# A hybrid encoder layer in fp32: the feed-forward's gate and up blocks taken in pairs, the norm's weights moved into h, one set of weight buffers

## The chip, the core and the metric

The kernel runs on one core of a Trainium2 chip. The metric is the device time of one execution in microseconds (us). PE is the matrix engine (TensorE), PEld its loads of stationary operands, DVE the vector engine (VectorE), ACT the scalar engine (ScalarE), POOL is GpSimd, and SP (SyncE) issues most transfers; SPq, PEq and so on are the queues of these engines.

## The reference

One layer over 256 tokens of width 2048, all in float32. What matters here:

```python
u = rms_norm(h, g_pre_mix);  proj = u @ w_in            # 2048 x 5120, three kinds of mixers behind it
h = h + rms_norm(mixed @ w_out, g_post_mix)             # 2048 x 2048
u = rms_norm(h, g_pre_ffn)
f = silu(u @ w_gate) * (u @ w_up)                       # 2048 x 5632 each
h = h + rms_norm(f @ w_down, g_post_ffn)                # 5632 x 2048
```

## The kernel before, in words

Activations are the stationary operand (128 x 128 tiles; two token tiles t = 0, 1) and weights the moving one (128 x 512). Every float32 product is made of three fp32r matmuls: high part by high part, high by low, low by high. So each weight block, an **item** of 256 rows x 512 columns (512 KB), takes 2 token tiles x 2 row tiles x 3 = 12 matmuls.

All items stand in one list, `stream`, in the order in which PE uses them: 80 of `w_in`, 32 of `w_out`, then the feed-forward's 11 blocks of 512 columns with 8 gate items and 8 up items each, then `w_down`. An item is loaded by SP into one of four raw buffers (`load`), cast to its high part `hi` by ACT and subtracted to its low part `lo` by DVE (`prep`) into one of five pairs, and taken by PE. In the feed-forward `prep` works in halves, since each row tile is scaled by its own column of `g_pre_ffn` (L240, L241); everywhere else one cast and one subtraction do the whole 128 x 1024 (L244, L246).

ACT, DVE and PE each run their instructions in the order in which the program writes them down (`manual_schedule`). Everything else (norms, mixers, silu, transposes) is written as side jobs, generators that are continued in `side.slot()` after each item as far as a budget of DVE and ACT time goes; `side.need(job)` continues slots until that job is written out, with no item of PE between.

In the down projection four pairs of k blocks (`SFORM`) are already done with seven products in place of eight (`seven`): the weights' sums are made by DVE (L226), the activations' sums in the feed-forward's last step.

Between `w_out` and the feed-forward stands a stretch written out by hand (the **h stage**): `h_part` makes h = x + normed output, `h_turn` transposes it on PE, `h_hi` casts it (ACT, out of PSUM), `h_lo` makes the low part (DVE). The gate items of block 0 are used there already. `h_job` then sums the squares of h on ACT (L418) for the norm's factor `rffn`. After the last up item `up_job` multiplies silu(gate) by up, transposes the result on PE and splits it for the down projection.

At the start `start_job` loads x transposed (`xT`, k tiles 8 to 11 and 12 to 15 as one transfer each) and then x itself in two halves.

Of the kernel before, what the change touches and what calls it, by code (L numbers as in the profile page):

```python
# [10 lines left out]
F32 = mybir.dt.float32  # L11
# [22 lines left out]
NRAW = 4  # L34
NPARTS = 5
# [25 lines left out]
class Side:  # L61
# [18 lines left out]
    def slot(self):  # L80
        self.n += 1
        self.left = [min(left + rate, self.MOST) for left, rate in zip(self.left, self.RATE)]
# [22 lines left out]
class Std:  # L105


    def __init__(self, ap, b=None, n=None):
        self.ap, self.b, self.n = ap, b, n
        self.has_load = True  # L110


class Prod:


    def __init__(self, group, name, ap, dst, add, frees):
        self.group, self.name, self.ap, self.dst, self.add, self.frees = group, name, ap, dst, add, frees
        self.has_load = ap is not None
        self.added = add is None


def seven(w11, w12, w21, w22, **at):

    g = {"bufs": {}, **at}
    return [
        Prod(g, "Q3", w22, "y", None, ""),  # L130
        Prod(g, "P7", w12, "x", ("x", "x", "y", ALU.add), ""),
        Prod(g, "P1", w11, "z", None, ""),
        Prod(g, "P6", None, "x", ("x", "x", "z", ALU.add), "z"),
        Prod(g, "P2", w21, "u", None, ""),
        Prod(g, "Q5", None, "y", ("y", "x", "y", ALU.subtract), "y"),
        Prod(g, "R4", None, "x", ("x", "x", "u", ALU.add), "xu"),
    ]

# [33 lines left out]
def block_kernel(ctx, tc, xT, x_tok, params, w_in, w_out, w_gate, w_up, w_down, lru_w, g_post, g_post2, out):  # L172
# [18 lines left out]
    for cs in ((6, 7), (0, 1, 2, 3), (4, 5)):  # L191
        stream += [w_out[b, c] for b in range(4) for c in cs]
    for i in range(NFB):
        stream += [w_gate[i, c] for c in range(8)] + [w_up[i, c] for c in range(8)]
    stream = [Std(ap) for ap in stream]
    gate0 = (len(mixers) + 4) * 8
    down0 = gate0 + NFB * 16
    plain = [n for n in range(NFK // 2) if n // 2 not in SFORM]
    downs = []
    for b, head, tail in ((0, 6, 4), (2, 3, 8)):  # L200
        prods = [p for i in SFORM for p in seven(*(w_down[b + c, 2 * i + k] for k, c in ((0, 0), (0, 1), (1, 0), (1, 1))), i=i)]
        downs.append(mingled(prods, [Std(w_down[b + c, n], b + c, n) for c in range(2) for n in plain], head, tail))
    stream += downs[0] + downs[1]
    early = range(gate0 + 1, gate0 + 1 + NEARLY)
    raws, parts = {}, {}
    at = {"load": 0, "prep": 0, "use": 0, "done": 0}

    sraws = Shelf([])

    def load(i, raw=None):  # L210
        item = stream[i]
        if isinstance(item, Prod):
            if item.has_load:
                buf = item.group["bufs"][item.dst] = sraws.lend(NT, CB)
# [5 lines left out]
    def add(i):  # L220

        item = stream[i] if i < len(stream) else None
        if isinstance(item, Prod) and not item.added and i < at["load"]:
            dst, a, b, op = item.add
            bufs = item.group["bufs"]
            V.tensor_tensor(out=bufs[dst], in0=bufs[a], in1=bufs[b], op=op)  # L226
            item.added = True

    def prep(i, tiles=None):
        item = stream[i]  # L230
        if isinstance(item, Prod):
            add(i)
            raw = item.group["bufs"][item.dst]
        else:
            raw = raws.pop(i)
        hi, lo = tiles or (wp.tile([P, 2, CB], F32R, tag=n, name=n, bufs=NPARTS) for n in ("hi", "lo"))
        if gate0 <= i < down0:
            for kk in range(2):
                g = pv("g_pre_ffn", (i - gate0) % 8 * 2 + kk)
                A.activation(hi[:, kk, :], raw[:, kk, :], AF.Copy, scale=g)  # L240
                V.scalar_tensor_tensor(out=lo[:, kk, :], in0=raw[:, kk, :], scalar=g, in1=hi[:, kk, :].bitcast(F32),  # L241
                                       op0=ALU.mult, op1=ALU.subtract)
        else:
            A.copy(out=hi, in_=raw)  # L244
            add(i + 1)
            V.tensor_tensor(out=lo, in0=raw, in1=hi.bitcast(F32), op=ALU.subtract)  # L246
        parts[i] = (hi, lo)
        if isinstance(item, Prod):
            for n in item.frees:
                sraws.back(item.group["bufs"].pop(n))  # L250

    def load_next():
        while at["load"] in early:
            at["load"] += 1
        if at["load"] < min(len(stream), at["prep"] + NRAW):
            item = stream[at["load"]]
            if isinstance(item, Prod) and item.has_load and not sraws.free:
                return False
            load(at["load"])
# [4 lines left out]
    def top_up_one():  # L264
# [10 lines left out]
        load_next()  # L275
        if i >= down0:
            while load_next():
                pass
# [11 lines left out]
    def release():  # L290
        at["done"] += 1
        top_up()

# [32 lines left out]
    later = const.tile([P, P], F32, name="later")  # L326
    G.affine_select(out=later, in_=ones, pattern=[[-1, P]], compare_op=ALU.is_ge, fill=0.0, base=0, channel_multiplier=1)
# [14 lines left out]
    xt = res.tile([P, NT, D], F32, tag="xt", name="xt")  # L342
# [1092 lines left out]
```

## Time and profile before

| | before |
|---|---|
| median of 3 runs | 1075.41 us (1074.4 to 1076.36) |
| the profiled execution's own time | 1075.32 us |
| its span | 1073.6 us |
| busy: PE, DVE, ACT | 1060.2, 769.4, 634.5 us |
| 128 x 512 matmuls written in the program | 4472 |

The span is what the trace covers; some 1.7 us of the execution lie around it. A PE row's busy time overlaps the next row's, since matmuls are pipelined: what a matmul costs is read from the distance between starts.

### The profile page before, as it was taken

To read this page: it belongs to the slowest core of one execution; us is meant where nothing else is said; L and a number is where in the kernel's file an instruction comes from. 1 tells how busy PE (TensorE), PEld (TensorE's weight loads), DVE (VectorE), ACT (ScalarE), POOL (GpSimd) and SP (SyncE) were. 2 spreads that over 40 slices of the span, in tenths; PEclk is the share of its full clock that TensorE was granted. 3 is DMA by queue.
4 is the path that set the end of the run, shared out by engine and by line. 5 is a ranking of instruction groups with operands and counts; after the bars stand their busy time and mean duration, and the time that the engine had idled before them with its cause. 6 is when DMAs were issued, how large, how long until landed. Compare 5 with 4: busy or idle time off the path is not lost.

```text
span 1073.6 us, 13241 instructions
## 1 busy us (share of the span) xinstructions
PE 1060.2 (99%) x4778; PEld 878.5 (82%) x4778; DVE 769.4 (72%) x1088; ACT 634.5 (59%) x901; POOL 7.8 (1%) x19
## 2 busy tenths in 40 slices
PE   8999999999999999999999999999999999999996
PEld 6888888888888888888888888888888888888885
DVE  6576998986688775765565665566655688788885
ACT  6778757678854855555464564555554455555552
POOL 0000000010000000000000000000000000000000
PEclk9999999999999999999999999999999999999998
DMA  8865554656563775565665556556556456656662
GB/s 313 279 197 175 193 169 153 194 167 215 204 230 104 248 234 185 177 206 185 196 185 188 196 183 193 193 177 197 194 191 237 162 197 223 230 170 196 223 230 79
DMA packets 58385, 211.21 MB, mean 197 GB/s; under 512 B 6480, under 2 KB 6864, under 8 KB 57552
## 3 DMA queue, kind: packets, MB, share of 16 engines
q1 hardware_dynamic: 58320, 210.38, 59.3%
q8 instruction: 37, 0.61, 0.2%
q14 instruction: 28, 0.23, 0.1%
HBM read 206.16 MB, written 4.19 MB: 196 GB/s over the span
## 4 chain that ended last, share of the span: by engine, by line
PE 96%; DMA 1%; DVE 1%; ACT 0%; SPq 0%; issue 0%; DVEq 0%; ACTq 0%
PE acc L297 24%; PE acc L298 24%; PE acc L299 24%; PE acc L1375 4%; PE acc L1374 4%; PE acc L1373 4%; PE bank L1375 3%; PE bank L1374 3%; PE bank L1373 3%; PE bank L1211 1%; DMA raw<-w_in 1%; DMA w<-xT 1%; PE bank L442 1%; DVE xt L1303 0%; PE bank L1065 0%; PE bank L752 0%
## 5 line engine op out<-in xcount | busy, mean ns | idle before, releaser
L297 PE MATMUL acc<-hi,w 128*128 128x512 f32 x1008 | 396.3, 393 | 1.5 <-DVE w L428 1.5
L298 PE MATMUL acc<-lo,w 128*128 128x512 f32 x1008 | 393.7, 391 | 0.3 <-DVE lo L861 0.3
L299 PE MATMUL acc<-hi,w 128*128 128x512 f32 x1008 | 393.6, 390 | 0.0
L241 DVE SCALAR_TENSOR_TENSOR lo<-raw,par,hi 128x512 fp32r<-128x512 f32 x344 | 242.8, 748 | 170.2 <-ACT hi L240 170.0
L240 ACT ACTIVATE hi<-raw,par 128x512 fp32r<-128x512 f32 x344 | 229.7, 718 | 193.2 <-PE acc L299 185.8
L246 DVE TENSOR_TENSOR lo<-raw,hi 128x1024 fp32r<-128x1024 f32 x166 | 202.2, 1225 | 85.9 <-ACT hi L244 84.5
L244 ACT CAST hi<-raw 128x1024 fp32r<-128x1024 f32 x166 | 172.5, 1048 | 127.6 <-PE acc L299 51.3
L297 PEld LDWEIGHTS acc<-hi,w 128*128 128x128 f32 x1008 | 189.9, 188 | 40.9 <-ACT hi L860 2.4
L299 PEld LDWEIGHTS acc<-hi,w 128*128 128x128 f32 x1008 | 189.8, 188 | 40.1 <-DVE w L1072 0.5
L298 PEld LDWEIGHTS acc<-lo,w 128*128 128x128 f32 x1008 | 189.8, 188 | 40.0 <-DVE lo L861 1.2
L244 ACT CAST hi<-w 128x1024 fp32r<-128x1024 f32 x56 | 58.6, 1053 | 41.7 <-DVE w L226 21.9
L246 DVE TENSOR_TENSOR lo<-w,hi 128x1024 fp32r<-128x1024 f32 x56 | 68.1, 1224 | 11.2 <-ACT hi L244 8.7
L1373 PE MATMUL acc<-hi,w 128*128 128x512 f32 x156 | 60.8, 390 | 0.0
L1375 PE MATMUL acc<-hi,w 128*128 128x512 f32 x156 | 60.7, 389 | 0.0
L1373 PE MATMUL bank<-hi,w 128*128 128x512 f32 x156 | 60.7, 389 | 0.0
L1374 PE MATMUL bank<-lo,w 128*128 128x512 f32 x156 | 60.7, 389 | 0.0
L1375 PE MATMUL bank<-hi,w 128*128 128x512 f32 x156 | 60.7, 389 | 0.0
L1374 PE MATMUL acc<-lo,w 128*128 128x512 f32 x156 | 60.7, 389 | 0.0
L684 DVE SCALAR_TENSOR_TENSOR w<-u,par,w 128x256 f32<-128x256 f32 x120 | 51.6, 492 | 0.0
L297 PE MATMUL acc<-hi,mh 128*128 128x512 f32 x128 | 50.4, 394 | 0.0
L299 PE MATMUL acc<-hi,ml 128*128 128x512 f32 x128 | 49.9, 390 | 0.0
L298 PE MATMUL acc<-lo,mh 128*128 128x512 f32 x128 | 49.8, 389 | 0.0
(252 smaller groups left out, 854.9 us busy)
## 6 DMA issues: line engine op xcount, KB each, us to landing
raw<-w_up SPq DMA_DIRECT2D x88, 512.0 KB, 3.5
raw<-w_gate SPq DMA_DIRECT2D x84, 512.0 KB, 4.1
raw<-w_in SPq DMA_DIRECT2D x78, 512.0 KB, 3.5
raw<-w_down SPq DMA_DIRECT2D x56, 512.0 KB, 3.5
raw<-w_out SPq DMA_DIRECT2D x32, 512.0 KB, 3.8
w<-w_down SPq DMA_DIRECT2D x32, 512.0 KB, 4.8
xt<-x_tok SPq DMA_DIRECT2D x2, 1024.0 KB, 8.1
w<-g_post SPq DMA_DIRECT2D x4, 512.0 KB, 5.3
```

What stands on the lines that cost most here:

```text
L240: A.activation(hi[:, kk, :], raw[:, kk, :], AF.Copy, scale=g)
L241: V.scalar_tensor_tensor(out=lo[:, kk, :], in0=raw[:, kk, :], scalar=g, in1=hi[:, kk, :].bitcast(F32), op0=ALU.mult, op1=ALU.subtract)
L244: A.copy(out=hi, in_=raw)
L246: V.tensor_tensor(out=lo, in0=raw, in1=hi.bitcast(F32), op=ALU.subtract)
L297: T.matmul(acc, xh(k)[:, ts], hi[:, kk, :], start=first, stop=False)
L298: T.matmul(acc, xh(k)[:, ts], lo[:, kk, :], start=False, stop=False)
L299: T.matmul(acc, xl(k)[:, ts], hi[:, kk, :], start=False, stop=last)
L442: T.transpose(out=b[:, c * P:(c + 1) * P], in_=src[:, t, c * P:(c + 1) * P], identity=ident)
L684: V.scalar_tensor_tensor(out=cy[:, n, :], in0=u[:, n, j:j + S], scalar=pv("dw_conv_w", j * 4 + n), in1=cy[:, n, :], op0=ALU.mult, op1=ALU.add)
L1373: T.matmul(out_bank, xhi, hi[:, kk, :], start=n == first[to] and kk == 0, stop=False)
L1374: T.matmul(out_bank, xhi, lo[:, kk, :], start=False, stop=False)
L1375: T.matmul(out_bank, xlo, hi[:, kk, :], start=False, stop=n == end[to] and kk == 1)
```

## The change

For blocks 1 to 10 the first 512 rows of the gate block and of the up block beside it are taken as one 2 x 2 matrix of 256 x 512 weight blocks (rows by gate/up) against the 2 x 2 of two token tiles by 256 rows of h, and multiplied with seven products (`seven_in_turn`): P1, P6, P7, Q5, P2, R4, Q3, each of 6 matmuls, in place of eight. That is 42 matmuls for 48, ten times: 4412 in the program for 4472. P1, P6 and P7 are running sums in one PSUM bank, which ACT copies out after each of them (L1397); P1, P6, P7 of a block are done among the up items of the block before. Sums of weights are made by DVE in `prep` (L259, 128 x 1024, four for each pair), sums of h once (`forms`).

For this h must hold the norm's weights itself, or the sums would mix rows with different weights. For columns 1024 to 2047 of h (b = 2, 3) `h_hi` now multiplies by `g_pre_ffn` on DVE (L1112) before the cast. For b = 0, 1 block 0 still runs with weights scaled in `prep`, and then `regain_job` rebuilds h from its two parts (L1255, DVE), scales it (L1258, ACT), splits it again, and for b = 0 makes the forms of h, all while the up items of block 0 run; P1 of block 1 is written behind both jobs (`side.need(*regain)`). Items of later blocks are split with one cast and one subtraction (L274, L276).

Raw buffers are one set, `weights`: four, and the three places of x once h is saved; a load may run six items ahead (`AHEAD`), and several are issued in one go. h is saved by GpSimd's queue. The forms of f go to DRAM and come back. x is loaded as four strips of columns.

```diff
-NRAW = 4
+AHEAD = 6
...
+def seven_in_turn(w11, w12, w21, w22, **at):
+    return dict([
+        item("P1", "z", "", ("z", w11), ("y", w22)),
+        item("P6", "z", "", ("x", w12), pre=[("x", "x", "y", ALU.add)], post=[("z", "z", "x", ALU.add)]),
+        item("P7", "x", ""),
+        item("Q5", "x", "x", pre=[("x", "z", "y", ALU.subtract)]),
+        item("P2", "u", "", ("u", w21)),
+        item("R4", "z", "zu", pre=[("z", "z", "u", ALU.add)]),
+        item("Q3", "y", "y"),
+    ])
...
+        if i:
+            q = sevens[i]
+            ffn += [*g[:2], q["Q5"], g[2], q["P2"], *g[3:5], q["R4"], g[5], q["Q3"]]
+        if i == 0:
+            q = sevens[1]
+            ffn += [*u[:6], q["P1"], u[6], q["P6"], u[7], q["P7"]]
+        elif i + 1 < NFB:
+            q = sevens[i + 1]
+            ffn += [*u[:-4], q["P1"], u[-4], q["P6"], *u[-3:-1], q["P7"], u[-1]]
...
-        if at["load"] < min(len(stream), at["prep"] + NRAW):
+        if i < min(len(stream), at["prep"] + AHEAD) and len(weights.free) >= len(stream[i].loads):
...
-        load_next()
-        if i >= down0:
-            while load_next():
-                pass
+        while load_next():
+            pass
...
     def h_hi(t, b):
-        A.copy(out=hh[b][:, :, t * P:(t + 1) * P], in_=turned[t, b].rearrange("p (c t) -> p c t", c=4))
+        bank = turned[t, b].rearrange("p (c t) -> p c t", c=4)
+        if b >= 2:
+            h = shelf.lend(4, P)
+            g = par[:, POFF["g_pre_ffn"] + 4 * b:POFF["g_pre_ffn"] + 4 * (b + 1)]
+            V.tensor_tensor(out=h, in0=bank, in1=g.rearrange("p (c t) -> p c t", t=1).broadcast_to([P, 4, P]), op=ALU.mult)
+            banks.back(turned[t, b])
+            bank = turned[t, b] = h
+        A.copy(out=hh[b][:, :, t * P:(t + 1) * P], in_=bank)
...
+    def forms(dst, a11, a12, a21, a22):
+        s1, s2, s3, s4 = (dst[:, n:n + 2, :] for n in (0, 2, 4, 6))
+        V.tensor_tensor(out=s1, in0=a21, in1=a22, op=ALU.subtract)
+        V.tensor_tensor(out=s2, in0=s1, in1=a11, op=ALU.subtract)
+        V.tensor_tensor(out=s4, in0=s2, in1=a12, op=ALU.add)
+        V.tensor_tensor(out=s3, in0=a11, in1=a21, op=ALU.subtract)
...
+    def regain_job(b):
+        while ("used", b) not in st:
+            yield WAIT
+        h = xplaces[b](4, S)
+        yield 1.2, 0, 0
+        V.tensor_tensor(out=h, in0=hh[b].bitcast(F32), in1=hl[b].bitcast(F32), op=ALU.add)
+        yield 0, 2.0, 0
+        for n in range(4):
+            A.activation(h[:, n, :], h[:, n, :], AF.Copy, scale=pv("g_pre_ffn", 4 * b + n))
+        yield 1.2, 1.05, 0
+        split(hh[b], hl[b], h)
+        if b == 0:
+            s = xplaces[2](8, P)
+            yield 1.9, 0, 0
+            forms(s, *quarters(h))
+            yield 1.0, 0.9, 0
+            split(*hform, s[:, 2:8, :])
+            yield 0.5, 0.4, 0
+            split(hh[0][:, 0:2, P:], hl[0][:, 0:2, P:], s[:, 0:2, :])
...
+    def ffn_after(item, full):
+        dst = {"P1": p1, "P6": p16, "Q5": q5}.get(item.name)
+        if item.name == "P7":
+            dst = p167[i % 2]
+        if dst is not None:
+            A.copy(out=dst, in_=accs[(i, 1, 1) if item.name == "Q5" else (i, 0, 1)])
...
+    run(ffn, ffn_uses, ffn_bank, ffn_after)
...
+    side.need(last_up)
```

On SP, at the start of the program: the two long transfers of xT (`w_196`, `w_232` before; `w_204`, `w_240` after) among the loads of `w_in`, each of which waits for the raw buffer that it fills. Before:

```order
L218 DMA raw_188<-w_in 128x1024 [waits DMAHW4_49,DVE_49]
L422 DMA w_196<-xT 128x1024 [waits DMAHW5_49]
L218 DMA raw_202<-w_in 128x1024 [waits DMAHW7_49,DMAHW6_49,DVE_49]
L218 DMA raw_208<-w_in 128x1024 [waits DMAHW1_49,DVE_49]
L422 DMA w_232<-xT 128x1024 [waits DMAHW0_49]
L218 DMA raw_238<-w_in 128x1024 [waits DMAHW3_49,DVE_49]
```

After:

```order
L252 DMA w_192<-w_in 128x1024 [waits DMAHW4_49,DVE_49]
L252 DMA w_194<-w_in 128x1024 [waits DMAHW7_49,DMAHW5_49,DVE_49]
L252 DMA w_196<-w_in 128x1024 [waits DMAHW6_49,DMAHW1_49,DVE_49]
L465 DMA w_204<-xT 128x1024
L252 DMA w_210<-w_in 128x1024 [waits DMAHW3_49,DMAHW0_49,DVE_49]
L252 DMA w_216<-w_in 128x1024 [waits DMAHW4_49,DVE_49]
L465 DMA w_240<-xT 128x1024 [waits DMAHW2_49]
```

The first xT transfer has moved behind two loads that wait for DVE, the second behind one that waits for a later step of DVE than before.

On ACT, in the up stage of block 0. Before, behind the gate's sigmoid (L1193) stand only the casts of the coming items, two halves each:

```order
L1193 ACTIVATE w_3377<-acc_3106,rffn_90 128x512 [waits DVE_49]
L1193 ACTIVATE w_3377<-acc_3107,rffn_90 128x512
L240 ACTIVATE hi_3399<-raw_3257,par_72 128x512 [waits DMAHW6_49,PE_49]
L240 ACTIVATE hi_3399<-raw_3257,par_72 128x512
L240 ACTIVATE hi_3421<-raw_3287,par_72 128x512 [waits DMAHW7_49,PE_49]
L240 ACTIVATE hi_3421<-raw_3287,par_72 128x512
L240 ACTIVATE hi_3441<-raw_3315,par_72 128x512 [waits DMAHW1_49,PE_49]
```

After, from the cast of P1's weights (`w_3319`, later P6's) to the first copy out of P1's bank (`acc_3531`). `w_3426` is h's columns 0 to 511 and `w_3477` columns 512 to 1023, `w_3434` the forms; `w_3343`, `w_3461` are up items 6 and 7, `w_3410` is P7's weights. Ahead of these rows stand the cast of up item 5 and the scaling and cast of `w_3426`:

```order
L274 CAST hi_3435<-w_3319 128x1024 [waits DMAHW7_49,PE_49]
L274 CAST hi_3455<-w_3343 128x1024 [waits DMAHW1_49,PE_49]
L1235 CAST w_3384<-w_3434 128x768 [waits DVE_49]
L274 CAST hi_3478<-w_3319 128x1024 [waits DVE_49,PE_49]
L1235 CAST w_3001<-w_3434 128x2x128 [waits Activation_49]
L1258 ACTIVATE w_3477<-w_3477,par_72 128x256 [waits DMASW1_49,DVE_49]
L1258 ACTIVATE w_3477<-w_3477,par_72 128x256 x3
L274 CAST hi_3501<-w_3461 128x1024 [waits DMAHW4_49,PE_49]
L1235 CAST w_3002<-w_3477 128x1024 [waits Activation_49]
L274 CAST hi_3525<-w_3410 128x1024 [waits PE_49]
L1397 COPY w_3386<-acc_3531 128x512 [waits PE_49]
```

The copy out of P1's bank, which PE needs before it can start P6 in that bank, stands behind a dozen other instructions, among them the whole second rebuild of h.

On PE, where the feed-forward ends: the transposes of the last f (L1211, L1306), from the bank `w_3377` or `w_3383`. Before, 48 matmuls of the down projection (L1373 to L1375; the last four are shown) stand between the last up item and them:

```order
L1375 MATMUL acc_7025<-hi_6991,w_3368 128x512
L1373 MATMUL acc_7025<-hi_6991,w_3357 128x512
L1374 MATMUL acc_7025<-lo_6992,w_3357 128x512
L1375 MATMUL acc_7025<-hi_6991,w_3368 128x512
L1211 MATMUL bank_7093<-ident_73,w_3377 128x128 [waits DVE_49,PE_49]
L1211 MATMUL bank_7093<-ident_73,w_3377 128x128 x3
L1211 MATMUL bank_7098<-ident_73,w_3377 128x128 [waits DVE_49]
L1211 MATMUL bank_7098<-ident_73,w_3377 128x128 x3
L1373 MATMUL acc_7024<-hi_7009,w_3359 128x512 [waits Activation_49]
```

After, with the last four matmuls of the last up item (L326 to L328, `acc_6668`), and behind them the first of the down projection (`acc_6962`):

```order
L328 MATMUL acc_6668<-hi_6823,w_2904 128x512
L326 MATMUL acc_6668<-hi_6823,w_3004 128x512
L327 MATMUL acc_6668<-lo_6824,w_3004 128x512
L328 MATMUL acc_6668<-hi_6823,w_2904 128x512
L1306 MATMUL bank_6932<-ident_73,w_3383 128x128 [waits DVE_49,PE_49]
L1306 MATMUL bank_6932<-ident_73,w_3383 128x128 x3
L1306 MATMUL bank_6937<-ident_73,w_3383 128x128 [waits DVE_49,PE_49]
L1306 MATMUL bank_6937<-ident_73,w_3383 128x128 x3
L326 MATMUL acc_6962<-hi_6841,w_3361 128x512 [waits Activation_49]
```

The transposes have moved up to stand directly behind the item whose result they turn.

## Rows read from the trace of the kernel before

**Rows 1.** Busy time of each engine, share of the span, instructions (the page's part 1).

```profile
PE 1060.2 (99%) x4778; PEld 878.5 (82%) x4778; DVE 769.4 (72%) x1088; ACT 634.5 (59%) x901; POOL 7.8 (1%) x19
```

**Rows 2.** PE's waits: line, releaser, us in total, times, longest.

```profile
PE acc L297 <- DVE w L428: 1.5, 1, 1.5
```

**Rows 3.** Timeline of PE: start us, us, line, out<-in (x8: eight in a row).

```profile
399.20 0.39 PE L297 MATMUL acc<-hi,w 128*128 128x512 f32 x1
399.43 0.39 PE L298 MATMUL acc<-lo,w 128*128 128x512 f32 x1
...
400.57 1.04 PE L1211 MATMUL bank<-ident,w 128*128 128x128 f32 x8
```

**Rows 4.** The chain in order of time: the transposes of two neighbouring blocks.

```profile
400.74 0.88 PE bank L1211 x8
...
445.14 0.88 PE bank L1211 x8
```

**Rows 5.** Costliest groups (part 5): line, shapes xcount | busy us, mean ns | idle before.

```profile
L241 DVE SCALAR_TENSOR_TENSOR lo<-raw,par,hi 128x512 fp32r<-128x512 f32 x344 | 242.8, 748 | 170.2 <-ACT hi L240 170.0
...
L246 DVE TENSOR_TENSOR lo<-raw,hi 128x1024 fp32r<-128x1024 f32 x166 | 202.2, 1225 | 85.9 <-ACT hi L244 84.5
L244 ACT CAST hi<-raw 128x1024 fp32r<-128x1024 f32 x166 | 172.5, 1048 | 127.6 <-PE acc L299 51.3
```

**Rows 6.** Busy us of each engine by stretch: h stage, feed-forward, down projection.

```profile
core 0: us, PE busy (x) PEld busy (x) DVE busy (x) ACT busy (x) POOL busy (x), PEclk, DMA share, GB/s
352.00:364.00 12.00, 12.00 (x61) 9.96 (x60) 12.00 (x19) 10.20 (x20) 0.00 (x0) 1.00 0.63 206
404.00:448.00 44.00, 44.00 (x200) 36.53 (x199) 26.00 (x39) 22.57 (x34) 0.00 (x0) 1.00 0.59 191
...
1020.00:1063.00 43.00, 43.00 (x191) 35.61 (x191) 31.45 (x41) 20.97 (x26) 0.00 (x0) 1.00 0.38 144
```

**Rows 7.** Timeline of SP's queue at the start.

```profile
8.84 0.52 SPq L422 DMA_DIRECT2D w<-xT  x1
11.34 3.67 SPq L218 DMA_DIRECT2D raw<-w_in  x2
15.06 0.43 SPq L422 DMA_DIRECT2D w<-xT  x1
```

**Rows 8.** Timelines of ACT, DVE and PE behind the second xT transfer.

```profile
22.17 1.71 ACT L430 ACTIVATE w<-w,par 128x256 fp32r<-128x256 f32 x4 [2.68 <-DMA w<-xT]
23.79 3.88 ACT L244 CAST hi<-raw 128x1024 fp32r<-128x1024 f32 x4
...
24.86 4.63 DVE L246 TENSOR_TENSOR lo<-raw,hi 128x1024 fp32r<-128x1024 f32 x4 [0.46 <-ACT hi L244]
...
20.23 0.39 PE L297 MATMUL acc<-hi,w 128*128 128x512 f32 x1
```

**Rows 9.** Timelines of ACT and DVE, PE at k tile 14: end of the h stage.

```profile
359.73 1.05 ACT L1068 CAST w<-bank 128x512 fp32r<-128x512 f32 x2
...
375.25 5.14 ACT L240 ACTIVATE hi<-raw,par 128x512 fp32r<-128x512 f32 x8
...
361.51 1.29 DVE L1072 TENSOR_TENSOR w<-bank,w 128x512 fp32r<-128x512 f32 x2
...
365.20 0.39 PE L297 MATMUL acc<-hi,w 128*128 128x512 f32 x1
```

**Rows 10.** Timelines of PE and DVE, windows (busy, PEclk, DMA share): PE's first and last matmuls.

```profile
9.51 0.63 PE L297 MATMUL acc<-hi,w 128*128 128x512 f32 x1
9.94 0.63 PE L298 MATMUL acc<-lo,w 128*128 128x512 f32 x1
...
1063.13 0.39 PE L1375 MATMUL bank<-hi,w 128*128 128x512 f32 x1
...
1064.24 0.68 DVE L1264 TENSOR_TENSOR w<-bank,w 128x512 f32<-128x512 f32 x1
...
1067.00:1070.00 3.00, 0.00 (x0) 0.00 (x0) 2.86 (x8) 0.00 (x0) 0.00 (x0) 0.50 0.24 89
```

More of the change, by code (lines that the diff above doesn't have):

```diff
@@ L34 @@
 NRAW = 4
+AHEAD = 6
+READ = ("P1", "P6", "P7", "Q5")
 NPARTS = 5
@@ L102, in need, with __init__ @@
             self.slot()
[L105 to L119, printed above, removed]
+class Item:
+    def __init__(self, bufs, loads, src, frees, pre=(), post=(), **where):
+        self.bufs, self.loads, self.src, self.frees = bufs, loads, src, frees
+        self.sums = {"pre": list(pre), "post": list(post)}
+        self.__dict__.update(where)
@@ L220, in add @@
[L220 to L227, printed above, removed]
+        for name, ap in item.loads:
+            item.bufs[name] = weights.lend(NT, CB) if raw is None else raw
+            nc.sync.dma_start(out=item.bufs[name], in_=ap)
@@ L237, in prep @@
[L237 to L242, printed above, removed]
+        sums(i, "pre")
+        sums(i, "post")
+        raw = item.bufs[item.src]
+        hi, lo = tiles or (wp.tile([P, 2, CB], F32R, tag=n, name=n, bufs=NPARTS) for n in ("hi", "lo"))
@@ L247, in prep @@
         parts[i] = (hi, lo)
-        if isinstance(item, Prod):
-            for n in item.frees:
-                sraws.back(item.group["bufs"].pop(n))
+        if not tiles:
+            weights.back(*(item.bufs.pop(n) for n in item.frees))
     def load_next():
@@ L292, in release, with six @@
         top_up()
+    def six(bank, tiles, w, first, last, again=False):
+        hi, lo = w
+        for kk in range(2):
+            xhi, xlo = tiles[kk]
+            T.matmul(bank, xhi, hi[:, kk, :], start=first and kk == 0, stop=False, skip_group_check=again)
+            T.matmul(bank, xhi, lo[:, kk, :], start=False, stop=False, skip_group_check=again)
+            T.matmul(bank, xlo, hi[:, kk, :], start=False, stop=last and kk == 1, skip_group_check=again)
     def product(acc, x, k, t, w, kk, first, last):
@@ L879, in block_kernel @@
     shelf.back(x0)
-    raws.clear()
+    weights.back(*(stream[i].bufs.pop("w") for i in range(2)))
     load_x(x1, 4, 2)
@@ new lines, in block_kernel, with ffn_uses, ffn_bank @@
+    accs, added = {}, {}
+    def ffn_uses(item):
+        if item.name is None:
+            return [((item.i, item.col, t), part_tiles(hidden, 2 * item.c, t)) for t in range(NT)]
+        to = {"P2": (0, 0), "Q3": (1, 0), "Q5": (1, 1)}.get(item.name, (0, 1))
+        return [((item.i, *to), of_product(item.name, hidden, hform))]
+    def ffn_bank(item, to):
+        if to not in accs:
+            i, col, _ = to
+            if i == 1 and col == 0:
+                side.need(*regain)
+            if i:
+                side.need(*(added[n] for n in ((i - 1, 0),) if n in added))
+                while col and ("up", i - 1) not in st:
+                    side.slot()
+            accs[to] = ps.tile([P, CB], F32, tag="acc", name="acc", bufs=4)
+        return accs[to]
@@ L1247, in block_kernel @@
+    added[0, 0] = side.add(0, silu_job(0, acc))
+    regain = [side.add(1, regain_job(b)) for b in range(2)]
+    run(ffn, ffn_uses, ffn_bank, ffn_after)
+    last_up = added[NFB - 1, 1]
     y2 = [[None] * 4 for _ in range(NT)]
@@ L1316, in std_form @@
[L1316 to L1327 removed]
+    sforms = {}
@@ new lines, in bring_back_job, with down_uses @@
+    def bring_back_job():
+        for b in (3, 0, 1, 2):
+            while b < 3 and xplaces[b] not in weights.free:
+                yield WAIT
+            if b < 3:
+                weights.free.remove(xplaces[b])
+            kept[b] = xplaces[b](NT, CB)
+            G.dma_start(out=kept[b], in_=hsave[b])
+        yield 0, 0, 0
+    yjobs, ybanks, sjobs = [], {}, {}
+    own = []
+    def down_uses(item):
+        if item.name is None:
+            return [((item.b, t), part_tiles(ff, 2 * item.n, t)) for t in range(NT)]
+        to = {"P2": (0, 0), "Q3": (1, 0), "R4": (0, 1)}.get(item.name)
+        four = [k for k in range(4 * item.i, 4 * item.i + 4)]
+        x = [lambda k, f=f: f(four[k]) for f in ff]
+        return [((item.b + to[0], to[1]) if to else (item.b, item.name), of_product(item.name, x, sforms[item.i]))]
@@ L1388, in block_kernel @@
+    bring, joined = [], set()
+    for n in range(2):
+        run(downs[n], down_uses, down_bank, down_after, NLAST * n)
+    acc = [ybanks[3, t] for t in range(NT)]
     for t in range(NT):
-        join_y(t, 3, bank[t, 1])
+        join_y(t, 3, acc[t])
         square_y(t, 3)
```

361 lines of the change are left out of this document (197 added, 164 removed).

## The prediction

> **What bounds the kernel now.** I read the page's busy shares first: PE is busy for 1060.2 of 1073.6 us, DVE for 769.4, ACT for 634.5 [rows 1]. Then PE's waits: the longest single one is 1.5 us [rows 2]. So PE's own matmuls set the time, and a matmul costs what lies between two starts: 399.20 to 399.43 on the timeline [rows 3]. A feed-forward block gives the finer number: from transposes to transposes are 445.14 - 400.74 = 44.40 us [rows 4], less 0.87 for the eight transposes, over 192 matmuls: 0.2267 us each. An item of 12 is 2.72 us, a product of 6 is 1.36.
>
> DVE and ACT wait for PE in most of the program, but not everywhere: in the h stage DVE is busy for 12.00 of 12.00 us, in a feed-forward block for 26.00 of 44, late in the down projection for 31.45 of 43, with no wait of PE there [rows 6]. So work added to DVE costs nothing in a block and everything in the h stage.
>
> **What the change takes away.** 60 matmuls by 0.2267: **-13.6 us**, if PE stays fed.
>
> **A steady block (blocks 1 to 10).** DVE's added work is four sums of 128 x 1024, five operations of 128 x 512, while the 128 x 512 halves of 0.748 become whole tiles of 1.225 [rows 5], 1.13 from start to start ((4.63 - 1.23) / 3) [rows 8]. A block then has 19 low parts and 4 sums by 1.13 (26 us), 9 operations by 0.6 to 0.7 (6) and the splits of f (3): 35 of 43 us. That is the load of the late down projection, where PE waits for nothing. Five pairs of `hi` and `lo` let the casts run more than 10 us ahead of PE, and P6 and Q5 follow the copies out of their bank with an item or more between. I cost it at **0**; if that cover went, each block would wait for its low parts (a rival below).
>
> **The start.** Before, the first long xT transfer was issued at 8.84 and the second at 15.06, landing 22.15 or so, since ACT scales it from 22.17 [rows 7, 8]. After, SP reaches the first one only behind two loads, the later of which waited until 15.0 before (they are the 3.67 us row at 11.34), so the first one takes the place of the second: issued at 15.06. With 0.5 MB less in flight I let it land at 21.4. Item 4 (k tiles 8, 9) was due at 20.23 [rows 8] and starts some 1.8 us late. Behind it ACT has four scalings (1.71) and the cast of item 5, as in the row at 22.17; that adds 0.3. The second transfer now stands behind a load that waits for item 4's low part, goes out at about 18.4 and, at 7.1 us again, lands at 25.5: scalings, cast and low part of item 6 end at about 28.3 + 1.2, against 28.5 when PE wants it: 1 more. Sum **+3** (1 to 6).
>
> **The h stage.** Four multiplications by the weights of 0.69 are put before the casts, on an engine without a gap. The casts of k tiles 12 to 15, two in a row at 359.73 before [rows 9], come after multiplication and cast in turn, at 363.3 and 365.2, the last low part at 366.4 where it was at 362.8 [rows 9]. PE gets k tiles 8, 9 some 1.4 us late and k tiles 12, 13 another 1.5: **+2.9** (2 to 5). ACT's list goes on only behind the last cast: the squares and casts behind it come about 6 us later, up item 5's cast at 381.6 where it stood at 375.25 [rows 9].
>
> **Block 0.** Without waits PE starts k tiles 14, 15 of the gate at 365.20 [rows 9], up item 5 ends 7 items later at 384.3, and P1, item 6, P6, item 7, P7 (9.5 us) end at 393.8; all of it 2.9 later by the h stage. Now the chain of `regain_job` in the order of the fence on ACT: low part of item 5 at 382.7 on DVE, silu's two (1.4), h's sum (1.2) to 386.4; four scalings (1.71), cast of h (1.05), cast of P1's weights (0.95) to 390.1; DVE's two low parts to 391.5. PE, free at 387.2, has P1 done only at 392.6: **+3.9**. Then DVE makes the forms (1.6), P7's sum and item 6's low part (2.3), to 395.4: item 6 ends 2.5 late. Then P6's sum, the forms' low part, P6's low part, two small ones and the second h sum: to 400.4. Four scalings, cast of item 7, cast of h, cast of P7's weights: 4.7, and only then the copy out of P1's bank (0.58): 405.7. PE was free at 397.9: **+7.7**. Sum **+14** (8 to 18): it shrinks one for one if the chain starts earlier, since every step stands in line on one of two engines.
>
> **After the longest wait.** [...] So I let the longest wait, that before P6, end in six matmuls at 0.43, as many as ran so from 9.51 on: **+1.2** (0 to 3).
>
> **The end of the feed-forward.** The transposes stand directly behind the last up item, and need a subtraction, an addition and a multiplication of 128 x 512 on DVE. DVE reads a finished bank 1.11 us after the last matmul's start (1063.13 to 1064.24) [rows 10], 0.88 past that matmul's slot; with 0.6, 0.6 and 0.75 behind it the first token tile can be turned after 2.8, and the second 0.65 later, of which its transposes hide 0.43: **+3** (2 to 4). Before, 48 matmuls covered it.
>
> **The rest.** Down projection: same items, same sums, one raw buffer less; forms come back from DRAM in a block's time: 0 (-1 to 2).
>
> Sum against the profiled execution's own 1075.3 (the median is 1075.4): 1075.3 - 13.6 + 3 + 2.9 + 14 + 1.2 + 3 = **1086 us**.
>
> **Rivals.**
> *The chain of block 0 is ready in time.* The place is the copy out of P1's bank; the price is the 14 + 1.2 us, and the point is a chain that starts by 368 instead of 382. For it: DVE has room near here, 26.00 us busy of 44 just behind this stretch [rows 6]. Against it: the first step stands behind item 5's low part, whose cast PE's progress allows only then. Time: 1086 - 15.2 = 1071. Chance 0.16.
> *Half of it.* ACT's lag of 6 us is made up by block 0, the chain starts 6 earlier, no clock lost: 1086 - 7.2 = 1079; with the start hidden too, 1076. Chance 0.11.
> *Steady blocks starve.* DVE at 35 of 43 us in line behind ACT, and one PSUM bank for P1, P6, P7; one us per block: 1096. For it: L246 and L241 wait for ACT in most of their idle time [rows 5]. Against it: the down projection. Chance 0.16.
> *The clock falls in every long wait.* In three waits of 2.5 us and more, and 14 matmuls slow each time (by 0.2): 3 x 2.8 - 1.2 = +7, 1093. Against it: in the rows the level fell only behind the end of all matmuls. Chance 0.07. [...]
>
> **How the numbers follow.** Chance of the forecast, 1080 to 1091 by the bounds of block 0 and the start: 0.50. The range 1070 to 1097 leaves out about 0.08 on each side. A difference of 0.2% (2.2 us) is what a measurement of this kernel tells from none: faster takes the first rival and a little of the second (0.17), same the middle of the second (0.07), slower the rest (0.76).
>
> **What would show it.** PE's waits: one of 7 to 8 us before P6 of block 1, released by ACT's copy; 3 to 4 before P1, released by DVE; 2 to 3 for the first low part behind it; 3 at the transposes of the last block; 2 and 1 at k tiles 8 and 12 of the first block. The spacing of blocks 2 to 10 is 43.0 us where it was 44.4. The prediction is wrong if PE's waits in block 0 sum to less than 8 us, or if the block spacing stays above 43.6.

## The result: 1.1% slower, and where the twelve microseconds came from

| | before | after |
|---|---|---|
| median | 1075.88 us (4 runs) | 1087.7 us (1087.13 to 1088.25, 4 runs) |
| ratio, with its 95% interval | | 1.0111 (1.0094 to 1.0129) |
| profiled execution's own time, span | 1075.32, 1073.6 us | 1087.62, 1085.9 us |

The forecast was 1086. In the page's first part PE has lost busy time and DVE has gained 80 us; both were meant, and neither is the loss (before: [rows 1]).

```profile
PE 1056.0 (97%) x4718; PEld 870.5 (80%) x4718; DVE 849.8 (78%) x1040; ACT 643.9 (59%) x819; POOL 21.9 (2%) x43
```

The loss stands in PE's waits. Before, the longest was 1.5 us [rows 2]; after, four groups hold a longer one, and the fifth row is the h stage (line, releaser, us in total, times, longest):

```profile
PE acc L326 <- issue: 6.1, 1, 6.1
PE acc L327 <- DVE lo L276: 3.2, 2, 2.2
PE bank L1306 <- DVE w L1299: 2.3, 1, 2.3
PE acc L326 <- ACT hi L274: 2.0, 1, 2.0
PE acc L333 <- ACT w L1115: 1.6, 2, 1.2
```

PE's timeline of block 0 says where (start, us, in brackets the idle time before and its releaser); its first row is the last matmul of up item 5. The four waits are those of P1 (391.96 and 393.41), of up item 6 (397.28) and of P6 (407.36):

```profile
389.58 0.39 PE L328 MATMUL acc<-hi,w 128*128 128x512 f32 x1
391.96 0.49 PE L326 MATMUL acc<-hi,w 128*128 128x512 f32 x1 [1.99 <-ACT hi L274]
393.41 0.50 PE L327 MATMUL acc<-lo,w 128*128 128x512 f32 x1 [0.95 <-DVE lo L276]
...
397.28 0.50 PE L327 MATMUL acc<-lo,w 128*128 128x512 f32 x1 [2.21 <-DVE lo L276]
...
400.68 0.63 PE L328 MATMUL acc<-hi,w 128*128 128x512 f32 x1
...
407.36 0.77 PE L326 MATMUL acc<-hi,w 128*128 128x512 f32 x1 [6.06 <-issue]
407.93 0.63 PE L327 MATMUL acc<-lo,w 128*128 128x512 f32 x1
...
411.77 0.58 PE L327 MATMUL acc<-lo,w 128*128 128x512 f32 x1
412.19 0.40 PE L328 MATMUL acc<-hi,w 128*128 128x512 f32 x1
```

The wait of P6 is put down to "issue", that is, to nothing that the profile shows. ACT's timeline shows it: the copy out of P1's bank (L1397) runs at 406.69, last in a row of scalings and casts without a gap, and P6 starts 0.1 us behind its end. Eleven matmuls behind that wait take 4.83 us (407.36 to 412.19) where 11 x 0.2267 is 2.49. From 383 to 407 ACT's timeline has no wait for a load and DVE's none either: each of the two waits for the other only.

```profile
402.25 1.70 ACT L1258 ACTIVATE w<-w,par 128x256 f32<-128x256 f32 x4 [2.46 <-DVE w L1255]
403.86 1.03 ACT L274 CAST hi<-w 128x1024 fp32r<-128x1024 f32 x1
404.80 1.04 ACT L1235 CAST w<-w 128x1024 fp32r<-128x1024 f32 x1
405.74 1.04 ACT L274 CAST hi<-w 128x1024 fp32r<-128x1024 f32 x1
406.69 0.57 ACT L1397 COPY w<-acc 128x512 f32<-128x512 f32 x1
```

The gain is there as well. In the chain of waits the transposes of blocks 1 to 9, 465.20 to 809.77, follow each other after 43.06 to 43.09 us, where it was 44.40 [rows 4], and PE waits for nothing in between; DVE is busy for 36.07 us of the first such distance (windows), 35 by the forecast.

```profile
465.20 0.87 PE bank L1306 x8
508.29 0.87 PE bank L1306 x8
551.35 0.87 PE bank L1306 x8
```

```profile
465.20:508.29 43.09, 43.09 (x197) 35.77 (x195) 36.07 (x40) 24.78 (x30) 1.06 (x2) 1.00 0.64 214
```

Two small losses stand ahead of block 0. The first channel transposes, a mark in both programs, come at 53.42 in the chain of before and at 55.65 after, with waits of 0.19 and 0.76 in front of the k tiles that need xT:

```profile
53.42 0.87 PE bank L442 x8
```

```profile
21.11 0.50 PE L333 MATMUL acc<-hi,w 128*128 128x512 f32 x1 [0.19 <-ACT w L473]
28.37 0.50 PE L334 MATMUL acc<-lo,w 128*128 128x512 f32 x1 [0.76 <-DVE lo L276]
...
361.10 0.50 PE L333 MATMUL acc<-w 128*128 128x512 f32 x1 [1.24 <-ACT w L1115]
367.02 0.49 PE L333 MATMUL acc<-hi,w 128*128 128x512 f32 x1 [0.36 <-ACT w L1115]
```

The last two rows are k tiles 8 and 12 of the gate in the h stage. Last, the end of the feed-forward, PE's timeline: the transposes wait for DVE, and seven matmuls behind them start 0.42 to 0.43 apart.

```profile
841.57 0.39 PE L328 MATMUL acc<-hi,w 128*128 128x512 f32 x1
844.22 1.29 PE L1306 MATMUL bank<-ident,w 128*128 128x128 f32 x8 [2.26 <-DVE w L1299]
...
846.35 0.63 PE L326 MATMUL acc<-hi,w 128*128 128x512 f32 x1
846.78 0.63 PE L327 MATMUL acc<-lo,w 128*128 128x512 f32 x1
```

Marks of both traces, one behind the other, give the account. The last up item of block 0 before P1 (item 5) ends at 389.81 where the forecast had 384.3 for a PE that never waits; P7, 9.52 us of work later, ends at 415.18, not 399.33; the last up item of all ends at 841.80, before at 833.95; the last matmul starts at 1075.21, before at 1063.13 [rows 10]. The row behind the last up item of before, and the last matmul of after:

```profile
833.95 0.39 PE L1373 MATMUL acc<-hi,w 128*128 128x512 f32 x1
```

```profile
1075.21 0.39 PE L328 MATMUL bank<-hi,w 128*128 128x512 f32 x1
```

| term | forecast | measured | from |
|---|---|---|---|
| 60 matmuls | -13.6 | -13.5 | what is left of 841.80 - 833.95 after the four terms below; by the block spacing it is 10 x (44.40 - 43.07) = 13.3 |
| start | +3 | +2.2 | 55.65 - 53.42 |
| h stage | +2.9 | +3.3 | 389.81 - 384.3 - 2.2 |
| block 0, its waits | +14 | +13.5 | 3.4 before P1, 2.4 in item 6, and 7.7 before P6, counted from where P6 would have started with all matmuls of item 6 0.2267 apart |
| slow matmuls behind P6 | +1.2 | +2.3 | 4.83 - 2.49 |
| end of the feed-forward | +3 | +4.2 | 1075.21 - 1063.13 - 7.85 |
| tail, the rest | 0 | +0.3 | 12.3 (1087.62 - 1075.32) less all above |

### The profile page after: what moved, and what is told of

It is laid out like the page before. It is cut to its first block, busy times and chain, and to the rows that moved or that the text cites. A ratio compares the mean times of both kernels' runs of the same rounds, so it can differ in the third digit from the quotient of the medians.

```text
span 1085.9 us, 13088 instructions
## 1 busy us (share of the span) xinstructions
PE 1056.0 (97%) x4718; PEld 870.5 (80%) x4718; DVE 849.8 (78%) x1040; ACT 643.9 (59%) x819; POOL 21.9 (2%) x43
## 4 chain that ended last, share of the span: by engine, by line
PE 91%; DVE 3%; ACT 3%; issue 1%; DMA 1%; SPq 0%; DVEq 0%; ACTq 0%
PE acc L327 17%; PE acc L326 17%; PE acc L328 17%; PE acc L333 9%; PE acc L334 9%; PE acc L335 9%; PE bank L326 3%; PE bank L327 3%; PE bank L328 3%; DMA w<-xT 1%; DVE lo L276 1%; PE bank L1306 1%; PE bank L485 1%; ACT hi L274 1%; ACT junk L461 0%
## 5 line engine op out<-in xcount | busy, mean ns | idle before, releaser
L276 DVE TENSOR_TENSOR lo<-w,hi 128x1024 fp32r<-128x1024 f32 x419 | 509.2, 1224 | 188.6 <-ACT hi L274 181.0
L274 ACT CAST hi<-w 128x1024 fp32r<-128x1024 f32 x419 | 436.4, 1051 | 315.5 <-PE acc L328 136.7
L326 PE MATMUL acc<-hi,w 128*128 128x512 f32 x820 | 322.7, 394 | 8.1 <-issue 6.1
L328 PE MATMUL acc<-hi,w 128*128 128x512 f32 x820 | 321.6, 392 | 0.0
L326 PEld LDWEIGHTS acc<-hi,w 128*128 128x128 f32 x820 | 155.2, 189 | 41.1 <-issue 6.7
L327 PEld LDWEIGHTS acc<-lo,w 128*128 128x128 f32 x820 | 155.3, 189 | 35.7 <-DVE lo L276 3.9
L328 PEld LDWEIGHTS acc<-hi,w 128*128 128x128 f32 x820 | 155.2, 189 | 32.4
L259 DVE TENSOR_TENSOR w<-w 128x1024 f32<-128x1024 f32 x72 | 87.7, 1218 | 0.0
L333 PEld LDWEIGHTS acc<-hi,w 128*128 128x128 f32 x336 | 63.8, 190 | 17.0 <-ACT hi L903 2.7
L334 PEld LDWEIGHTS acc<-lo,w 128*128 128x128 f32 x336 | 63.8, 190 | 15.3 <-DVE lo L276 1.6
L335 PEld LDWEIGHTS acc<-hi,w 128*128 128x128 f32 x336 | 63.7, 190 | 14.7 <-DVE w L1119 1.3
L326 PE MATMUL bank<-hi,w 128*128 128x512 f32 x168 | 65.4, 390 | 0.0
L327 PE MATMUL bank<-lo,w 128*128 128x512 f32 x168 | 65.4, 389 | 0.0
L328 PE MATMUL bank<-hi,w 128*128 128x512 f32 x168 | 65.4, 389 | 0.0
```

What stands on the lines that cost most here:

```text
L259: V.tensor_tensor(out=item.bufs[dst], in0=item.bufs[a], in1=item.bufs[b], op=op)
L326: T.matmul(bank, xhi, hi[:, kk, :], start=first and kk == 0, stop=False, skip_group_check=again)
L327: T.matmul(bank, xhi, lo[:, kk, :], start=False, stop=False, skip_group_check=again)
L328: T.matmul(bank, xlo, hi[:, kk, :], start=False, stop=last and kk == 1, skip_group_check=again)
L333: T.matmul(acc, xh(k)[:, ts], hi[:, kk, :], start=first, stop=False)
L334: T.matmul(acc, xh(k)[:, ts], lo[:, kk, :], start=False, stop=False)
```

## The experiments

Theory: PE's waits come from single chains of steps that stand in order on ACT and DVE, while both engines have time to spare; at the start and at the end two more orders cost the rest. Rivals: the engines' load itself makes the waits, so that a wait only moves; or the waits are those of transfers.

### e1_start: the loads at the start in the order of before

```diff
-        if i < min(len(stream), at["prep"] + AHEAD) and ...
+        ahead = AHEAD if at["prep"] > 9 else NRAW
+        if i < min(len(stream), at["prep"] + ahead) and ...
...
-        while load_next():
+        while load_next() and at["prep"] > 9:
             pass
```

> One part undone: until ten items are split, loads run four items ahead and one at a time, as before, so the two long transfers of xT stand on SP's queue where they stood. Theory A (each wait of PE is worth what it shows): the first channel transposes come back from 55.65 to 53.4 us and all later ones move with them; time 1087.7 - 2.2 = 1085.5. Theory B (a later wait takes up what an earlier one gives back, since ACT and DVE then have less lead): the transposes of block 0 at 420.8 move by less than 1 us and the time stays within 1 us of 1087.7.

1084.51 us, ratio to before 1.0086 (1.0071 to 1.0101). SP issues the two xT transfers at 9.84 and 14.62 (after: 14.46 and 17.75), PE waits at neither k tile, and the first channel transposes come at 54.18 where they came at 55.65. What came back stayed: the transposes of block 0 are 2.17 earlier (418.62), the last matmul 2.14, about 1.5 by the start, and 0.7 since only eight matmuls behind P6's wait were slow (3.46 us, 405.93 to 409.39), where it had been eleven (4.83). The profiled execution was the slowest of the four (1085.46), so the trace accounts for its 2.2 us and not for the whole 3.2 of the median. Of the start's 2.2 us the order of the loads made 1.5 (the means of all runs with either order, given below, lie as far apart); what is left (54.18 against 53.42) comes with a wait of 1.38 at PE's first item, for which no order was tried.

### e2_end: other work of PE between the last up item and the last transposes

```diff
-    side.need(last_up)
-    spots = [...]
+    def bring_forms():
+        side.need(last_up)
+        spots = [...]
...
+            if item.name and not sforms:
+                bring_forms()
```

> One part undone: the last block's transposes are written behind the first plain items of the down projection, up to its first product, where before they were asked for as well. The trace of the change has 2.6 us of waiting in front of them and then nine matmuls 0.43 apart. Theory A: both go, 2.6 + 1.7 = 4.3 us, time 1083.4, and the granted clock stays at 1.00 behind 840 us. Theory B: the down projection, which starts with less lead then, waits for its weights or for the forms out of DRAM instead, and less than 2 us come back.

1083.32 us, 1.0076 (1.0061 to 1.0091). The last matmul starts at 1070.94, 4.27 earlier, with no wait there and a granted clock of 1.00 from 840 to 850 (0.83 after; seven matmuls there, not nine, started 0.42 to 0.43 apart). So the end's 4.2 us was the place of the transposes, slow matmuls included.

### e7_twice: one scaling more in front of the copy

```diff
             A.activation(h[:, n, :], h[:, n, :], AF.Copy, scale=pv("g_pre_ffn", 4 * b + n))
+        if b == 1:
+            junk = small.tile([P, CB], F32, tag="junk", name="junk", bufs=1)
+            for n in range(4):
+                A.activation(junk[:, :S], h[:, n, :], AF.Copy, scale=pv("g_pre_ffn", 4 * b + n))
```

> The change with one cost doubled: ACT scales the second rebuild's four parts twice (the second time into a scratch tile that nobody reads), 1.7 us more ahead of the copy out of P1's bank. Theory A (PE waits for that copy, which stands in ACT's list behind the rebuild): P6 starts 1.7 us later, at about 409.1, and the time is 1089.4. Theory B (PE's 6.1 us there, which the profile calls issue, are for something else, a load, the forms or P6's weights): P6 starts where it did, 1087.7.

1088.92 us, 1.0123 (1.0106 to 1.014). PE's timeline: the wait has grown by 1.9, and the transposes of block 0 stand at 422.82 where they stood at 420.79. P6 starts only 1.45 later than in the changed kernel, since up item 5 ended 0.58 earlier in this execution. The 1.2 us in the median are hardly more than the scatter of the executions; the trace carries the reading: what the profile calls "issue" is ACT's list.

```profile
408.81 0.76 PE L326 MATMUL acc<-hi,w 128*128 128x512 f32 x1 [7.95 <-issue]
```

### e3_copy: the second rebuild behind the copy of P1's bank

```diff
-        while ("used", b) not in st:
+        while ("used", b) not in st or b and "P1 read" not in st:
...
-                side.need(*regain)
+                side.need(regain[0])
...
+        if item.name == "P1":
+            st["P1 read"] = True
+        if i == 1 and item.name == "P7":
+            side.need(regain[1])
```

> Only an order is changed: the second rebuild of h (columns 512 to 1023) is written behind the copy out of P1's bank, not ahead of it. Theory A (PE waits for P6's bank because ACT works through its list in order): the copy ends near 402.3 in place of 407.3, P6 starts 5 us earlier, item 7 takes some of the rest, and 5 us come back: 1082.7. Theory B (the wait, which the profile puts down to issue and not to ACT, is for P6's weights or for the forms, or it moves whole to the first gate item of block 1, which needs the second rebuild): P6 starts less than 1 us earlier, or the first gate item of block 1 waits 4 us or more; the time stays above 1086.

1084.46 us, 1.009 (1.0073 to 1.0107). The copy runs at 402.43 and P6 starts at 403.11, 4.25 earlier, but P7 now waits for the next copy, behind the rebuild that was put off:

```profile
403.11 0.47 PE L326 MATMUL acc<-hi,w 128*128 128x512 f32 x1 [1.42 <-issue]
...
410.36 0.50 PE L326 MATMUL acc<-hi,w 128*128 128x512 f32 x1 [2.90 <-ACT w L1397]
```

The transposes gain 1.7 us (419.08), the time 3.2; in the profiled execution (1084.31) the rest is the end of the feed-forward, where no matmul was slow. The expectation of 5 us failed: a step that is put off in a list is still in it.

### e4_nofirst: block 1 without the seven products, its first rows last

```diff
-    for i in range(1, NFB):
+    for i in range(2, NFB):
...
-            q = sevens[1]
-            ffn += [*u[:6], q["P1"], u[6], q["P6"], u[7], q["P7"]]
+            ffn += u
...
+        if item.i == 1 and item.name is None and item.col == 0 and item.c in (0, 2):
+            side.need(regain[item.c // 2])
```

Block 1 takes eight products here (6 matmuls more), and its gate and up begin with rows 1024 to 2047. Where its second token tile should read the first rows of h, it reads one of h's forms; that part of the output is another one.

> The first pair is taken away: blocks 2 to 10 use seven products, block 1 runs its eight items each of gate and up, in the order of k tiles 8 to 15 and then 0 to 7, so that nothing of block 0's rebuild of h is wanted before its four first items are through. Theory A: the 15.9 us of waits and slow matmuls in block 0 go, six matmuls (1.4 us) come back: 1087.7 - 14.5 = 1073.2. Theory B: DVE, with 80% of a block's time already in use, has not made up the rebuild by block 2; waits of 3 us or more stand in blocks 1 or 2, and the time is above 1077.

1079.64 us, 1.0038 (1.0023 to 1.0053): 8 us better than the change, 6 worse than expected. Of the 6, one is the start (first channel transposes at 56.69 for 55.65); 4.7 stand in up item 6, the two stops below and slow matmuls behind them (0.41 to 0.43 apart from 395.22 to 397.76). The waits of P1 are now those of up item 6, of the same length to 0.01 us, since its cast stands behind the first rebuild whatever comes next on PE:

```profile
393.17 0.50 PE L327 MATMUL acc<-hi,w 128*128 128x512 f32 x1 [2.00 <-ACT hi L275]
394.62 0.80 PE L328 MATMUL acc<-lo,w 128*128 128x512 f32 x1 [0.95 <-DVE lo L277]
```

### e5_all: e1, e2 and e4 together, each rebuild two items later

```diff
-        while ("used", b) not in st:
+        while ("used", b + 1) not in st:
...
+            while "first rows" not in st:
+                yield WAIT
             yield 0.5, 0.4, 0
             split(hh[0][:, 0:2, P:], hl[0][:, 0:2, P:], s[:, 0:2, :])
```

The last form of h is now split only when block 1 has read the first rows, and the whole layer is computed. Of block 1 only the gate keeps e4's order of k tiles.

> Three parts together: the start's order of loads, the late transposes, and block 1 with its eight items as in the run without the first pair, where the pause in front of up item 6 of block 0 stayed because the first rebuild of h stood ahead of that item's cast on ACT. Here each rebuild is written two items later, behind the casts of the block's last items, and the form that overwrites h's first rows only when block 1 has read them. Theory A (the waits are separate and add): 1087.7 - 2.2 - 4.2 - 15.9 + 1.4 = 1066.8, no wait of PE over 0.5 us between 370 us and the end. Theory B (DVE and ACT, at their share, must spend the rebuild's time somewhere): waits of 3 us or more in sum appear in blocks 1 or 2, time above 1070.

1071.15 us, 0.9958 (0.9943 to 0.9973): faster than before, and 4 us short of theory A. PE still waits 1.62 at 395.22 and 0.29 and 0.76 from 401.04 on, for casts and low parts that stand behind a rebuild: 2.7 us on the record, some 3.5 from start to start, where the matmul behind the first and the third wait takes 0.34 to the next start and not 0.23. Theory B had 3 us or more and a time above 1070, so this is its side: the waits had moved.

### e6_hlate: all four parts of h rebuilt late, none in the h stage

```diff
-        return range(2 * c, 2 * c + 2) if c < 4 else None
+        return range(2 * c, 2 * c + 2)
...
-        if b >= 2:
-            h = shelf.lend(4, P)
-            ...
-            bank = turned[t, b] = h
...
-    regain = [side.add(1, regain_job(b)) for b in range(2)]
+    regain = [side.add(1, regain_job(b)) for b in range(4)]
```

Each rebuild is written behind the last use of the next part, as in e5; block 1's items stand in their usual order again.

> As the run with three parts together, and all of h is rebuilt late: no multiplication by the norm's weights in the h stage, the weights of all items of block 0 scaled in halves as before, four rebuilds in place of two, across blocks 0 and 1. Theory A (the four multiplications in the h stage cost PE 3.2 us): that stage comes back to the time of before and the program to 1066.8 - 3.2 = 1063.6. Theory B (the two added rebuilds, 5 us of DVE and 5.5 us of ACT within ten items, are too many): ACT is late by block 1, PE waits there for 2 us or more, and the time is not under 1066.

1070.59 us, 0.9951 (0.9936 to 0.9966). The waits of the h stage are gone, and the rebuilds give them back in block 1. Three times PE stops twice, for the cast (L1231) and the low part (L1232) of a rebuilt h, 4.5 us in all. The first pair on PE's timeline:

```profile
397.66 0.50 PE L328 MATMUL acc<-hi,w 128*128 128x512 f32 x1 [0.91 <-ACT w L1231]
...
399.11 0.50 PE L330 MATMUL acc<-hi,w 128*128 128x512 f32 x1 [0.63 <-DVE w L1232]
```

Yet neither engine is full: in the window of these waits DVE is busy for 15.88 and ACT for 17.07 of 24 us.

```profile
394.00:418.00 24.00, 19.53 (x84) 14.37 (x83) 15.88 (x16) 17.07 (x26) 0.00 (x0) 1.00 0.56 188
```

They wait for each other in turn. ACT stands idle for 4.12 us until DVE has made the sum, then scales and casts; DVE stands idle for 2.71 until the item's cast, which is queued behind the scaling, is done:

```profile
402.67 1.71 ACT L1254 ACTIVATE w<-w,par 128x256 f32<-128x256 f32 x4 [4.12 <-DVE w L1251]
404.29 1.03 ACT L275 CAST hi<-w 128x1024 fp32r<-128x1024 f32 x1
...
401.43 1.21 DVE L1251 TENSOR_TENSOR w<-w 128x1024 f32<-128x1024 f32 x1
405.35 1.23 DVE L277 TENSOR_TENSOR lo<-w,hi 128x1024 fp32r<-128x1024 f32 x1 [2.71 <-ACT hi L275]
```

### e9_early: e6, with sum and scaling ahead of the rebuilds

Only the cast and the low part overwrite what block 0 still reads. The sum of h's two parts and the scaling go to other memory and can be written out earlier. With that, the cast and the low part are allowed right behind the last use of their part again, not one part later as in e6; no run separates these two moves.

```diff
+    def scaled_job():
+        for b in range(4):
+            h = xplaces[b](4, S)
+            yield 1.2, 0, 0
+            V.tensor_tensor(out=h, in0=hh[b].bitcast(F32), in1=hl[b].bitcast(F32), op=ALU.add)
+            yield 0, 2.0, 0
+            for n in range(4):
+                A.activation(h[:, n, :], h[:, n, :], AF.Copy, scale=pv("g_pre_ffn", 4 * b + n))
+            scaled_h[b] = h
...
-        while ("used", min(b + 1, 3)) not in st or b == 3 and ("regained", 2) not in st:
+        while ("used", b) not in st or b not in scaled_h:
...
+    side.add(1, scaled_job())
+    regain = [side.add(2, regain_job(b)) for b in range(4)]
```

> The run before this one (all rebuilds of h late, 1070.59 us) still lost 4.5 us of TensorE in front of the rebuilds in block 0, with ScalarE idle 4.1 us behind VectorE and VectorE idle 2.7 us behind ScalarE. Here the sum of the squares and the scaling of each part of h are written among up items 0 to 5 of block 0, so that only the cast and the low part stay behind the last use of the form before. Theory A: the waits came from the two engines waiting for each other in turn at each rebuild, sum, scaling, cast, low part; with the first two off that chain they go, nearly all: 1066 us (1064.5 to 1067.5), waits of TensorE in block 0 under 1.5 us in sum. Theory B: the two engines have no room in that stretch, whatever the order; the scalings then delay the casts of the up items beside them, the waits only move ahead, into up items 3 to 9, and the time is 1069 us or more.

1064.63 us, **0.9896 (0.9879 to 0.9914)** of before: the fastest version here. All of PE's waits from block 0 on are one of 0.35 us. The same instructions for h as in e6, in another order, now keep both engines busy for 24.5 of 28 us, and PE doesn't wait for them (windows):

```profile
374.00:402.00 28.00, 27.65 (x126) 22.52 (x125) 24.53 (x33) 24.63 (x38) 0.00 (x0) 1.00 0.61 206
```

On ACT a scaling stands between the casts of two items, without the waits of e6:

```profile
376.24 1.70 ACT L1254 ACTIVATE w<-w,par 128x256 f32<-128x256 f32 x4
377.84 1.33 ACT L271 ACTIVATE hi<-w,par 128x512 fp32r<-128x512 f32 x2
379.07 1.70 ACT L1254 ACTIVATE w<-w,par 128x256 f32<-128x256 f32 x4
380.67 1.33 ACT L271 ACTIVATE hi<-w,par 128x512 fp32r<-128x512 f32 x2
```

It keeps 54 of the 60 matmuls, since block 1 takes eight products. 54 x 0.2267 = 12.2 us, of which 11.4 (1076.06 - 1064.63) are in the time.

### e10_scaled: the changed kernel with this one edit

`scaled_job` as above for the two parts that the change rebuilds, and nothing else; P1, P6 and P7 stay in block 0.

> One edit to the changed kernel alone: the sums and the scalings of h's first two parts stand ahead of the casts of up item 5 and of P1's weights, and only cast, low part and forms stay where the rebuilds were; the order of the items, the start and the end are the change's own. Theory A (the chain across ScalarE and VectorE made the waits of block 0, step by step): the second scaling of 1.7 us and the wait of 2.5 us for its sum leave ScalarE's list ahead of the copy out of P1's bank, which moves from 406.7 to about 401; item 6's low part comes 2 us earlier; up item 5 loses up to 1 us. P6 starts at 401 to 402 where it was 407.4, the wait there is 3 to 4 us, and the time is 1081.5 us (1079.5 to 1083). Theory B (the two engines' share of work in the stretch makes the waits): the work is the same, so P6 stays within 2 us of 407.4 and the time above 1085.

1079.95 us, 1.004 (1.0026 to 1.0055), 7.8 us less than the change. The rows of ACT and PE show the steps of the forecast, shortened: the copy at 399.82 and not 406.69, P6 at 400.49 and not 407.36, P1's wait 0.43 and not 2.9; only item 6 waits as before for its low part, behind forms and sums on DVE.

```profile
390.68 0.50 PE L328 MATMUL acc<-hi,w 128*128 128x512 f32 x1 [0.43 <-DVE w L1236]
394.55 0.67 PE L327 MATMUL acc<-lo,w 128*128 128x512 f32 x1 [2.43 <-DVE lo L276]
400.49 0.47 PE L326 MATMUL acc<-hi,w 128*128 128x512 f32 x1 [1.57 <-issue]
```

```profile
397.92 1.99 ACT L274 CAST hi<-w 128x1024 fp32r<-128x1024 f32 x2
399.82 0.57 ACT L1404 COPY w<-acc 128x512 f32<-128x512 f32 x1
```

The transposes stand at 412.44, 8.35 us earlier than after. The waits up to the end of P7 (406.07) are 6.8 us where they were 13.5, no matmul behind P6 is slow (2.3 us after), and a new stop in block 1 takes 0.8 back. This is the fastest execution of the five (1077.7; the others took 1079.39 to 1080.18), so its trace shows about 2 us more gain than the median. The share of work is the same, so the load of the two engines did not make the 6.7 us that went. For what stayed this run does not decide: ahead of item 6's low part, and behind it up to 396.50, DVE works without a wait from 385.72 on.

## Why the prediction was right, point by point

- **What bounds the kernel, and the gain.** Right: every matmul taken away in a steady block came off the time. The spacing is 43.06 to 43.09, forecast 43.0; the rival of starving blocks is out, with DVE at 36 of 43 us and no wait.
- **Block 0.** Right in place, order and size: 3.4, 2.4 and 7.7 us against 3.9, 2.5 and 7.7. e7 showed that the copy's place in ACT's list sets P6; e10 that sum and scaling in the chain were worth 6.7 of the 13.5 us; how far the other 6.8 are order and how far DVE's load stays open. One releaser was off: the first 1.99 us of P1's wait were for ACT's cast, the second part for DVE.
- **After the longest wait.** Right in place, not in size. No run shows the term of six matmuls and 1.2 us, the author's estimate from the first matmuls of the program [rows 10]; in its place eleven matmuls behind the wait of 6.06 us were slow, 2.3 us in all. The rival that had the clock fall in every long wait came out in part: slow matmuls followed the stops of 2.21, 6.06 and 2.26 us (six, eleven and seven, where the rival assumed 14 each time), none those of 1.99 and 0.95. In windows of 1 us the granted clock is 0.50 from 399 to 401 with PE at work, 1.00 from 402 to 405 with PE idle, and 0.50 from 406 to 412: it fell in the long wait, but only after it had risen in the same wait, and it had fallen before in item 6.
- **The end of the feed-forward.** Mis-sized by 1.2 us: the wait came near the forecast (2.4 from slot to start where 2.8 was taken, 0.2 for the second token tile as taken), but the slow matmuls behind it had not been costed (1.6).
- **The start.** 2.2 for 3. The first transfer went out at 14.46 (forecast 15.06), the second at 17.75 (18.4), so k tile 8 started 0.9 late (21.11 for 20.23) and not 1.8. Part of the loss was not of the named kind: PE was already 0.5 late when it got there, behind an idle time of 0.62 in its first item.
- **The h stage.** 3.3 for 2.9, with the waits at k tiles 8 and 12, as named (from start to start 1.8 and 1.5, forecast 1.4 and 1.5); the cast of up item 5 at 383.39 (forecast 381.6 plus the late start).
- **The sum.** 1086 for 1087.7. The two errors that matter, 1.1 and 1.2 us, are both slow matmuls, and the start gave 0.8 back.

Open stays what makes PE's first item late, and why kernels with the same start differ there: the first channel transposes come at 55.09 to 56.69 in the six kernels with the change's order of loads (mean 55.72), at 53.61 to 54.83 in the four with that of before put back (mean 54.24).

## What to carry to other kernels

- When a step needs two engines in turn, its length is the sum of its parts on both, with what stands ahead of each part in either list, and the engines' share does not show it: in e6 both were idle for about 30% of the stretch and PE still waited 4.5 us. Split such a step at what it overwrites, and write the part that overwrites nothing as early as its inputs exist.
- Before a product is taken out of a steady loop, look at the first round of the loop: here it gained 13.5 us in ten rounds, and the change into the new form took 15.8 us out of the round before it.
- Where a profile gives a wait to "issue", look at what ended just then on the engine that must release the buffer, and at what stands ahead of it in its list.

## What the runs showed of the hardware

**The same short pause cost more than its length in some runs, and not in others.** Behind the same pause of 2.26 us before the last transposes, the changed kernel has seven matmuls 0.42 to 0.43 apart, e4 seven, e1 five, and e3, e7 and e10 none, with the same instructions there; the granted clock of 840 to 850 is 0.83 after and 1.00 in e3. It is worth 1.6 us: from the transposes to the twelfth matmul behind them are 5.23 us after and 3.64 in e3. Behind the longer wait of P6 the count varied too: eleven after (a wait of 6.06 us), nine in e2 (5.49), eight in e1 (5.82), fourteen in e7 (7.95), all of them 0.34 to 0.57 apart. So two kernels of this case differ by that much without a reason in their edits: in the profiled executions 0.7 us of e1's gain and 1.6 of e3's and of e10's are of this kind.

**The clock also fell inside an item.** After waits of 1.99, 0.95 and 2.21 us with seven matmuls among them, the last six of up item 6 ran 0.43 apart (400.68 is the last), at a granted clock of 0.50 from 399 to 401. They cost nothing of their own, since P6 started 0.1 us behind ACT's copy.
